# Tying the modulation products of a partial-product stage to its own products, and spreading a norm two half tiles later

## The chip, the core and the metric

The kernel is one program on one core of a Trainium2 chip. The core has a matrix engine (TensorE, PE in the profile, with its weight loads as PEld), a vector engine (DVE), a scalar engine (ACT), a general engine (GpSimd, POOL) and a queue that issues transfers from memory (SyncE, SP). The metric is the device time of one launch in microseconds (us), the median over runs of the same program. For the kernel before it is 3037.05 us over three runs, which lay between 3035.22 and 3038.11.

Each engine works through its own list of instructions in a fixed order. That order is made when the program is compiled: a scheduler goes through the instructions as the Python program emitted them, estimates when each would be ready, and puts an instruction ahead of one emitted earlier where the earlier one would still have to wait. An ordering can be forced with `tc.issue_after(ins)`: every instruction emitted inside the block on the engine of `ins` then comes behind `ins` in that engine's list. It is an order alone, not a wait.

## What is computed

The reference is a two-layer backbone over 256 latent and 256 context tokens with 2048 channels. Layer 0 mixes tokens by pooling, layer 1 by neighbourhood attention, and each is followed by a gated feed-forward network (FFN) with 5504 hidden channels. All of it is in float32. What matters here is layer 0:

```python
ml = (silu_c @ w_mod[i] + b_mod[i]).reshape(B, 6, 1, D)
a_lat = modulate(rms_norm(h, norm1_g[i]), ml[:, 0], ml[:, 1])
y_lat = pool_mix(a_lat, pool_w[j], pool_b[j], pool_scale[j])
h = h + ml[:, 2] * y_lat
h = h + ml[:, 5] * conv_ffn(modulate(rms_norm(h, norm2_g[i]), ml[:, 3], ml[:, 4]),
                            ffn_w_gate[i], ffn_w_up[i], ...)
```

The modulation `silu_c @ w_mod` is a product of one vector per stream with about 100 MB of weights per layer, so it is mostly a matter of fetching weights. Two streams (latent and context) go through the same weights. The second RMS norm needs the sum of squares over all 2048 channels of the mixed `h`, so its scale is known only when the last channel group is mixed.

## The kernel before

**The partial stage.** The mixer works on four groups of 512 channels. As soon as a group is mixed, its share of the first FFN products can be computed, without waiting for the others and without the norm's scale, which is multiplied in later. The loop `for g in range(4)` (L745) does this for the first eight gate and up columns (`NS = 8`). For each group, `partial` (L660) runs 16 tiles: eight gate or up columns in two blocks of four, gate before up. One tile is 12 products, in four triples over the group's channel blocks `A[4g]` to `A[4g+3]` (L705 to L707; `cg` and `cu` in the profile). A half tile is six of them. `between(half)` (L754) is called before each half tile, numbered 0 to 31 in a group, and emits everything else that has to happen meanwhile.

**The modulation.** `mod_pe` (L227) makes one chunk of 512 modulation channels: four pieces, each of two weight tiles of 512 KB (`wm` in the profile). Every second piece it emits one set of eight modulation products (L240, `mod`), called a pair below because it covers two pieces; the profile counts 16 records for it, because each instruction is recorded twice. After the fourth piece ACT copies the sum out (L255, `modev`), and four transposes (L262, `modt`) and small DVE operations finish the chunk's vector. For the last three chunks (`ch > 20`) there is one set of four products for each piece. `need(n)` pushes this generator to its n-th step; `between` calls it with a count that grows by about five for every eight half tiles. In group `g` the shift that the product `pw` (L687) reads is done at step `20 * g + 21`.

The list `behind_of` (L224) holds instructions behind which `mod_pe` puts its products and transposes. The mixer of the first group fills it; it is cleared before the partial stage (L741), so that within the partial stage the scheduler may put modulation products anywhere.

**Loads and rooms.** All weights go through one SP queue in the order of the program. They land in rooms: six tiles of their own and some tiles of `A` lent for a time (`LENT`, `lend`). A load waits until the last reader of its room is done, and all later loads wait behind it.

**Banks.** Products land in banks of PSUM. The tag `d` has three, used in turn by the tiles of `cg` and `cu`, by `pw`, by the transposes (`modt`, `ptg`, `ptu`) and by the norm. The modulation products have one bank of their own (`m`).

**The second norm.** In the last group (`g == 3`), before half tile `NRH` = 3, `n2.rstd()` (L377) emits the whole of the norm's end: 16 small products that sum the squares over partitions (L382, `n2s`), a reduction and a scaling on DVE (L385, L386), a power on POOL (L387, `n2v`), four diagonals on DVE (L390, `n2d`), and one product that spreads them over all partitions (L392, `n2b`). ACT copies that into `rstd` (L759). `need(20 * g + 21)` follows. From then on `normalise` makes the FFN's input of one channel block every second half tile (L403, L405, L406), twelve blocks within the stage and the last four after it, and `late` multiplies stored partial products by the scale on POOL (L461).

Of the kernel before, what the change touches and what calls it, by code (L numbers as in the profile page):

```python
# [17 lines left out]
P = 128  # L18
# [41 lines left out]
def kernel(ctx: ExitStack, tc: tile.TileContext, xT, cxT, wmod, wg, wu, wd, wp,  # L60
# [263 lines left out]
    class Norm:  # L324
# [50 lines left out]
            return pb  # L375

        def rstd(self):  # L377
            nj = self.n // P
            ps = bank("d", f"{self.name}s")
            for i, sq in enumerate((self.acc, self.last)):  # L380
                for j in range(nj):
                    nc.tensor.matmul(ps[:, 2 * j + i : 2 * j + i + 1], sq[:, P * j : P * j + P], ones[:, 0:1],  # L382
                                     start=True, stop=True)
            v = main.tile([P, 4], F32, tag="normv", bufs=2, name=f"{self.name}v")[:, :nj]
            nc.vector.tensor_reduce(out=v, in_=ps[:, 0 : 2 * nj].rearrange("p (j a) -> p j a", a=2), axis=AX.X, op=ALU.add)  # L385
            nc.vector.tensor_scalar(v, v, 1.0 / D, EPS, op0=ALU.mult, op1=ALU.add)  # L386
            nc.gpsimd.tensor_tensor(v, v, minus_half[:, :nj], op=ALU.pow)  # L387
            dg = self.pool.tile([P, 512], F32, tag="t2", name=f"{self.name}d")
            for j in range(nj):
                nc.vector.tensor_scalar(dg[:, P * j : P * j + P], ident, v[:, j : j + 1], None, op0=ALU.mult)  # L390
            pb = bank("d", f"{self.name}b")
            nc.tensor.matmul(pb[:, : self.n], ones, dg[:, : self.n], start=True, stop=True)  # L392
            return pb

    A = {}
# [34 lines left out]
    with ExitStack() as ph0:  # L430
# [64 lines left out]
        with ExitStack() as phs:  # L495
# [50 lines left out]
            def need(n):  # L546
                while done[0] < n:
                    next(pump0, None)
                    done[0] += 1
# [110 lines left out]
            def partial(g, sh, between):  # L660

                step = 0
                for fa in range(0, NS, 4):
                    for q, (nm, wsrc) in enumerate((("g", wg), ("u", wu))):
# [12 lines left out]
                        for j in range(4):  # L677
                            f = fa + j
                            between(2 * step)
                            if j == (3 if fa == 0 and q == 0 else 0):  # L680
                                need(20 * g + 21)
                                assert g in READY
                                pw = bank("d", f"pw{nm}{g}_{fa}")
                                for i in range(4):
                                    for jj, (t, n) in enumerate(ts):
                                        t3 = t.rearrange("p (f c) -> p f c", c=512)
                                        nc.tensor.matmul(pw[32 * i : 32 * i + 32, 256 * jj : 256 * jj + 256], sh[:, i, :],  # L687
                                                         t3[:, :, P * i : P * i + P], start=True, stop=True,
                                                         tile_position=(0, 32 * i))
                                ev = f0.tile([P, 512], F32, tag="t2", name=f"pe{nm}{g}_{fa}")  # L690
                                nc.scalar.copy(ev, pw)
                                used(ts)
                            if f >= NC:
                                if g == 0:
                                    HELD[f, q] = bank("gu", f"c{nm}_{f}")
                                ps = HELD[f, q]
                                first, final = g == 0, g == 3
                            else:
                                ps = bank("d", f"c{nm}{g}_{f}")
                                first = final = True  # L700
                            hi, lo = parts[j // 2]
                            for i in range(4):
                                c = 512 * (j % 2) + P * i
                                xh, xl = flat(A[4 * g + i][:, 0]), flat(A[4 * g + i][:, 1])
                                nc.tensor.matmul(ps, hi[:, c : c + P], xh, start=(first and i == 0), stop=False)  # L705
                                nc.tensor.matmul(ps, hi[:, c : c + P], xl, start=False, stop=False)
                                nc.tensor.matmul(ps, lo[:, c : c + P], xh, start=False, stop=(final and i == 3))  # L707
                                if i == 1:
                                    between(2 * step + 1)
                            step += 1  # L710
                            if f >= NC:
                                continue
                            if g == 0:
                                if q == 0:
                                    PART[f] = act_tile(f"part{f}", F32)
                                nc.scalar.copy(PART[f][:, q], ps)
                            else:
                                nc.vector.tensor_tensor(PART[f][:, q], PART[f][:, q], ps, op=ALU.add)
# [26 lines left out]
            for g in range(4):  # L745
                if g < 3:
                    lend((range(8, KT), [*range(12, KT), *range(4)], range(8))[g])
                mix = mixer(g + 1) if g < 3 else None
                todo = [20 * g + 20 + n for n in STEPS] if g < 3 else []
                last = [14]  # L750
                F = {}
                rstd = n2.acc

                def between(half):  # L754
                    need(min(20 * g + LEAD + RATE * (half + 1) // 32, 20 * g + LEAD + PMAX))
                    if (g, half) in LENT:
                        lend(LENT[g, half])
                    if g == 3 and half == NRH:
                        nc.scalar.copy(rstd, n2.rstd())  # L759
                        late_norm.append(rstd)  # L760
                        need(20 * g + 21)
                    if todo and done[0] > todo[0] and half >= last[0] + 2:
                        last[0] = half
                        todo.pop(0)
                        next(mix)
                    k = (half - NRH) // 2
                    if g == 3 and 0 <= k < 12 and (half - NRH) % 2 == 0:
                        normalise(0, 3, h_of, both, rstd, f0, range(k, k + 1), keep=F)
                    if g == 3 and half == 24:
                        EARLY[NC] = late(NC, (0,))[0]  # L770
                    if g == 3 and half in GATES:
                        e = GATES.index(half)
                        acts[e], _ = gate0(e, *late(e))

                partial(g, shs[g % 2], between)
                for n in todo:
                    need(n)
                    next(mix)
            need(97)
            in_turn.clear()  # L780
            nbank[0] = 0
            A.update(F)
# [766 lines left out]
```

## Time and profile before

| What | us |
|---|---|
| median of three runs | 3037.05 |
| the profiled execution, its own time | 3037.08 |
| its span, first to last instruction | 3035.3 |
| TensorE busy in the span | 2972.4 (98%) |
| DVE busy | 1943.6 (64%) |
| ACT busy | 1380.5 (45%) |
| POOL busy | 833.1 (27%) |

The profile gives times in us from the start of the span. A row of a timeline has the start, the length, the engine, the line, the operation, what it writes and reads, and, in square brackets, how long the engine stood idle before it and what ended that. A row of a window has the length of the window, the busy time of PE, PEld, DVE, ACT and POOL with the number of instructions in brackets, the granted TensorE clock as a share of full speed, the share of time in which the DMA engines were busy, and GB/s. Rows of the chain of waits have a start, a length and a name.

### The profile page before, as it was taken

How to read it: one execution, taken by the hardware profiler on the slowest of the kernel's cores; microseconds unless marked ns; L12 is line 12 of the kernel's file. 1: busy time of each engine (PE TensorE's matmuls, PEld its weight loads, DVE VectorE, ACT ScalarE, POOL GpSimd, SP SyncE). 2: the span in 40 equal slices, each digit the busy share in tenths (PEclk: the TensorE clock that was granted, in tenths of full speed). 3: DMA queues.
4: the chain of work that ended last, by engine and by line, in shares of the span. 5: the costliest groups of instructions: out<-in, count | busy, mean ns of one | idle time of the engine just before them, and what ended most of it. 6: DMA issues, size and time to landing. Idle time of an engine off the chain costs nothing.

```text
span 3035.3 us, 40942 instructions
## 1 busy us (share of the span) xinstructions
PE 2972.4 (98%) x15132; PEld 2414.0 (80%) x15132; DVE 1943.6 (64%) x2782; ACT 1380.5 (45%) x2237; POOL 833.1 (27%) x819
## 2 busy tenths in 40 slices
PE   5999999999999999999999999999999999999998
PEld 2666568888888888888888887878888888888887
DVE  5455664386584857758485657474778666666666
ACT  4433454323333242333434534343556666566665
POOL 0000213303123030311305002020002566566665
PEclk9999999999999999999999999999999999999999
DMA  9798563374665847566482333333345555555563
GB/s 395 290 366 306 209 209 103 109 252 146 208 197 168 245 140 236 156 205 203 156 254 82 127 100 122 107 120 112 106 158 195 185 193 191 190 183 187 183 192 119
DMA packets 178935, 561.81 MB, mean 185 GB/s; under 512 B 17712, under 2 KB 22576, under 8 KB 178736
## 3 DMA queue, kind: packets, MB, share of 16 engines
q1 hardware_dynamic: 178736, 559.19, 56.5%
q8 instruction: 120, 1.97, 0.3%
q14 instruction: 79, 0.65, 0.1%
HBM read 557.03 MB, written 2.10 MB: 184 GB/s over the span
## 4 chain that ended last, share of the span: by engine, by line
PE 88%; issue 6%; DMA 2%; POOL 1%; DVE 1%; ACT 1%; SPq 0%; DVEq 0%; POOLq 0%; ACTq 0%
PE d L863 5%; PE d L864 5%; PE d L865 5%; PE u L1070 5%; PE g L1070 5%; PE d L1123 4%; PE g L807 4%; PE g L805 4%; PE g L806 4%; PE u L807 4%; PE u L805 4%; PE u L806 4%; PE u L1073 3%; PE g L1073 3%; PE d L1127 2%
## 5 line engine op out<-in xcount | busy, mean ns | idle before, releaser
L876 POOL TENSOR_TENSOR hl<-hl,dy 128x256 f32<-128x256 f32 x160 | 146.1, 913 | 945.8 <-ACT dy L875 945.6
L1139 POOL TENSOR_TENSOR hl<-hl,dy 128x256 f32<-128x256 f32 x320 | 332.1, 1075 | 188.3 <-ACT dy L1137 186.0
L300 DVE SCALAR_TENSOR_TENSOR macc<-wm,sc,macc 128x512 f32<-128x512 f32 (+1 forms) x360 | 328.7, 943 | 75.3 <-DMA wm<-wmod 74.3
L875 ACT ACTIVATE dy<-d,modT 128x256 f32<-128x256 f32 x320 | 133.1, 469 | 187.3 <-PE d L865 168.9
L876 POOL TENSOR_TENSOR hc<-hc,dy 128x256 f32<-128x256 f32 x160 | 129.4, 809 | 0.0
L174 DVE TENSOR_TENSOR wd_2l<-wd,wd_2h 128x1024 fp32r<-128x1024 f32 (+1 forms) x44 | 55.7, 1271 | 108.1 <-ACT wd_2h L172 106.9
L1137 ACT ACTIVATE dy<-d,modT 128x512 f32<-128x512 f32 x160 | 104.5, 684 | 43.0 <-PE d L1127 41.4
L240 PE MATMUL mod<-wm,sc 128*32 128x512 f32 x768 | 99.6, 629 | 9.9 <-DMA wm<-wmod 9.9
L1225 POOL TENSOR_TENSOR rk<-rk,rp 128x256 f32<-128x256 f32 x16 | 14.8, 926 | 324.0 <-DVE rk L1224 225.6
L174 DVE TENSOR_TENSOR wd_3l<-wd,wd_3h 128x1024 fp32r<-128x1024 f32 (+1 forms) x44 | 53.4, 1234 | 77.1 <-ACT wd_3h L172 75.7
L635 POOL TENSOR_TENSOR hl<-hl,pz 128x256 f32<-128x256 f32 x12 | 9.8, 820 | 286.9 <-ACT pz L633 286.9
L174 DVE TENSOR_TENSOR wd_1l<-wd,wd_1h 128x1024 fp32r<-128x1024 f32 (+1 forms) x44 | 53.7, 1225 | 53.3 <-ACT wd_1h L172 53.3
L172 ACT CAST wd_1h<-wd 128x1024 fp32r<-128x1024 f32 (+1 forms) x44 | 45.3, 1031 | 72.3 <-PE u L806 47.1
L174 DVE TENSOR_TENSOR wd_0l<-wd,wd_0h 128x1024 fp32r<-128x1024 f32 (+1 forms) x44 | 54.5, 1247 | 36.9 <-ACT wd_0h L172 36.9
L1314 ACT ACTIVATE sb<-sb,nm 128x512 f32<-128x512 f32 x64 | 46.3, 723 | 58.9 <-DVE nm L1310 57.3
L172 ACT CAST wd_0h<-wd 128x1024 fp32r<-128x1024 f32 (+1 forms) x44 | 45.0, 1031 | 54.5 <-PE u L1070 29.1
L1102 DVE TENSOR_TENSOR actb<-sgb,actb 128x256 fp32r<-128x256 f32 x43 | 50.8, 1180 | 26.0 <-ACT actb L1101 26.0
L480 ACT ACTIVATE sg<-g 128x512 f32<-128x512 f32 x43 | 27.2, 632 | 88.4 <-DVE g L477 88.3
L863 PE MATMUL d<-act,wd_2h 128*128 128x512 f32 x172 | 67.1, 390 | 0.0
L864 PE MATMUL d<-act,wd_2h 128*128 128x512 f32 x172 | 66.9, 389 | 0.0
L865 PE MATMUL d<-act,wd_2l 128*128 128x512 f32 x172 | 66.9, 389 | 0.0
L864 PE MATMUL d<-act,wd_0h 128*128 128x512 f32 x172 | 66.9, 389 | 0.0
(1778 smaller groups left out, 9304.8 us busy)
## 6 DMA issues: line engine op xcount, KB each, us to landing
wm<-wmod SPq DMA_DIRECT2D x384, 512.0 KB, 6.5
wd<-wd SPq DMA_DIRECT2D x168, 512.0 KB, 4.4
wg<-wg SPq DMA_DIRECT2D x156, 512.0 KB, 4.7
wu<-wu SPq DMA_DIRECT2D x156, 512.0 KB, 4.6
wv<-wv SPq DMA_DIRECT2D x32, 512.0 KB, 4.0
wk<-wq SPq DMA_DIRECT2D x32, 512.0 KB, 3.9
wq<-wq SPq DMA_DIRECT2D x32, 512.0 KB, 3.8
wo<-wo SPq DMA_DIRECT2D x32, 512.0 KB, 4.4
```

The lines of the kernel that those rows point to most:

```text
L174: eng.tensor_tensor(lo[:, :n], t[:, :n], hi[:, :n].bitcast(F32), op=ALU.subtract)
L300: nc.vector.scalar_tensor_tensor(acc[s], v, sc2[:, k, s : s + 1], acc[s], op0=ALU.mult, op1=ALU.add)
L805: nc.tensor.matmul(ps, hi[:, c : c + P], xh, start=(k == 0), stop=False)
L806: nc.tensor.matmul(ps, hi[:, c : c + P], xl, start=False, stop=False)
L807: nc.tensor.matmul(ps, lo[:, c : c + P], xh, start=False, stop=(k == KT - 1))
L863: nc.tensor.matmul(ps, hi[:, o : o + P], xh, start=(i == 0), stop=False)
L864: nc.tensor.matmul(ps, hi[:, o : o + P], xl, start=False, stop=False)
L865: nc.tensor.matmul(ps, lo[:, o : o + P], xh, start=False, stop=(i == n - 1))
L876: nc.gpsimd.tensor_tensor(h_of(s)[:, k, :], h_of(s)[:, k, :], y[:, s], op=ALU.add)
L1070: nc.tensor.matmul(ps, hi[:, c : c + P], flat(B[k]), start=(k == 0), stop=False)
L1073: nc.tensor.matmul(ps[:, T:], lo[:, c : c + P], B[k][:, 0], start=False, stop=(k == KT - 1))
L1139: nc.gpsimd.tensor_tensor(hl[:, k, :], hl[:, k, :], y[:, q], op=ALU.add)
```

## The change

It has two parts. First, `partial` writes into `behind_of` the last product of each triple as it is emitted, so that modulation products and their transposes come behind the partial product that precedes them in the program. The list is cleared after the stage. Second, the norm's end is cut in two. The sums, the power and the diagonals are still emitted before half tile 3, and `need(20 * g + 21)` now follows them directly. The spreading product and the copy into `rstd` are emitted before half tile 5, with the spreading product behind the partial product before it. Each `normalise` step of the last group is emitted two half tiles later: the first before half tile 5 instead of 3, the twelfth before 27 instead of 25.

```diff
         def rstd(self):
+            self.diagonal()
+            return self.spread_all()
+
+        def diagonal(self):
             nj = self.n // P
...
                 nc.vector.tensor_scalar(dg[:, P * j : P * j + P], ident, v[:, j : j + 1], None, op0=ALU.mult)
+            self.dg = dg
+
+        def spread_all(self, last=()):
             pb = bank("d", f"{self.name}b")
-            nc.tensor.matmul(pb[:, : self.n], ones, dg[:, : self.n], start=True, stop=True)
+            with ExitStack() as behind:
+                for x in last:
+                    behind.enter_context(tc.issue_after(x))
+                nc.tensor.matmul(pb[:, : self.n], ones, self.dg[:, : self.n], start=True, stop=True)
             return pb
...
-                                nc.tensor.matmul(ps, lo[:, c : c + P], xh, start=False, stop=(final and i == 3))
+                                ins = nc.tensor.matmul(ps, lo[:, c : c + P], xh, start=False, stop=(final and i == 3))
+                                behind_of[:] = [ins.ins]
...
                     if g == 3 and half == NRH:
-                        nc.scalar.copy(rstd, n2.rstd())
+                        n2.diagonal()
+                        need(20 * g + 21)
+                    if g == 3 and half == NRH + 2:
+                        nc.scalar.copy(rstd, n2.spread_all(behind_of))
                         late_norm.append(rstd)
-                        need(20 * g + 21)
...
-                    k = (half - NRH) // 2
+                    k = (half - NRH) // 2 - 1
...
             need(97)
+            behind_of.clear()
             in_turn.clear()
```

## The prediction

> **What bounds the kernel now.** I read the page first (busy time by engine), then windows over the groups of the partial stage, then the chain of waits around the second norm, then the timelines of PE, DVE and ACT there. The page's first block, and windows over the third group, the last group in pieces, and the handover to the FFN:
>
> ```profile
> PE 2972.4 (98%) x15132; PEld 2414.0 (80%) x15132; DVE 1943.6 (64%) x2782; ACT 1380.5 (45%) x2237; POOL 833.1 (27%) x819
> ```
>
> ```profile
> 245.00:326.00 81.00, 80.60 (x472) 52.93 (x464) 46.50 (x91) 27.01 (x47) 2.86 (x4) 1.00 0.86 322
> 326.00:417.00 91.00, 82.93 (x478) 48.70 (x478) 63.95 (x123) 46.01 (x94) 22.14 (x17) 0.96 0.69 238
> ...
> 341.00:351.00 10.00, 5.82 (x23) 1.82 (x23) 3.81 (x8) 2.28 (x3) 1.02 (x1) 0.66 0.98 340
> ...
> 357.00:413.00 56.00, 55.62 (x315) 33.71 (x317) 45.36 (x84) 32.44 (x65) 15.32 (x10) 1.00 0.66 230
> ...
> 419.00:430.00 11.00, 11.00 (x43) 8.86 (x43) 11.00 (x21) 8.88 (x18) 0.00 (x0) 0.85 0.64 196
> ```
>
> PE bounds the kernel, and the stage too: 80.60 of 81 us in the third group, while the transfers have room (0.86). The last group takes 91 us with less mixing in it, and its loss sits in one place: from 341 to 351 PE is busy for 5.82 us at a clock of 0.66. The chain of waits there, then PE's timeline:
>
> ```profile
> 334.01 11.08 DMA wm<-wmod
> ...
> 345.18 3.64 PE mod L240 x16
> 348.82 1.95 PE n2b L392 x2
> ```
>
> ```profile
> 327.13 3.64 PE L240 MATMUL mod<-wm,sc 128*32 128x512 f32 x32
> 330.70 0.66 PE L721 MATMUL ptu<-ident,peu 128*128 128x128 f32 x4
> 331.12 0.70 PE L705 MATMUL cg<-Ad,wcg_0h 128*128 128x512 f32 x2
> ...
> 338.61 1.92 PE L240 MATMUL mod<-wm,sc 128*32 128x512 f32 x16
> 345.18 3.64 PE L240 MATMUL mod<-wm,sc 128*32 128x512 f32 x16 [4.64 <-DMA wm<-wmod]
> 348.75 2.02 PE L392 MATMUL n2b<-n2d,ones 128*128 128x512 f32 x2
> 350.61 0.60 PE L262 MATMUL modt<-ident,modev 128*128 128x128 f32 x4
> 350.96 0.48 PE L705 MATMUL cg<-Ad,wcg_0h 128*128 128x512 f32 x1
> ...
> 355.63 1.09 PE L687 MATMUL pwg<-wcg,sh 128*32 128x256 f32 x16 [1.65 <-ACT A L405]
> ...
> 361.20 0.50 PE L705 MATMUL cu<-Ad,wcu_0h 128*128 128x512 f32 x1
> ...
> 366.55 0.39 PE L707 MATMUL cu<-Ad,wcu_0l 128*128 128x512 f32 x1
> ```
>
> After two tiles (24 products, 331.12 to 338.61 with the norm's 16 sums) come two pairs of chunk 20. In the program they belong before half tiles 6 and 9, behind 36 and 54 products. The scheduler hoisted them; the second had no data until 345.09 (334.01 + 11.08), and the spread, the transposes of chunk 15 and the third tile stand behind it. Those transposes come late too: the chunk's last pair ended at 330.77, but their bank apparently follows the spread's in turn, and `pw` then waits 1.65 us for the shift they make.
>
> **The change, part by part.** Unit prices from these rows: a product is 5.35 / 23 = 0.233 us (361.20 to 366.55, 23 steps), so a tile is 2.8; a pair at full clock is about 1.85 (the 327.13 row: two in 3.64); transposes before a product 0.35 (350.61 to 350.96). Spreading costs 1.05 at full clock, by the first norm's spread:
>
> ```profile
> 26.65 1.12 PE L392 MATMUL n1b<-n1d,ones 128*128 128x512 f32 x2
> 27.70 1.92 PE L240 MATMUL mod<-wm,sc 128*32 128x512 f32 x16
> ```
>
> *The last group, cost first.* The 327.13 row is both pairs of chunk 15. The second belongs behind 18 products, so the tie takes it out of the place where PE waited for this group's channels anyway:
>
> ```profile
> 329.46 0.50 ACT L645 ACTIVATE Ad<-hc,modT 128x256 fp32r<-128x256 f32 x1
> ...
> 333.77 0.47 DVE L646 SCALAR_TENSOR_TENSOR Ad<-hc,modT,Ad 128x256 fp32r<-128x256 f32 x1
> ```
>
> PE is free at 327.13 + 1.85 + 0.42 (`ptu`) = 329.4, and the first product can start at 329.46 + 0.50 = 330.0. The low parts end at 334.24, when 18 products (4.2 us) are through, so DVE does not hold them. Then 24 products (5.6), the sums (7.49 - 5.6 = 1.9) and the pair (1.85) end at 339.35, where they ended at 338.61 before: 0.75 us lost.
>
> *The last group, gain.* From there: transposes of chunk 15 (0.35), the third tile (2.8), the first pair of chunk 20 (1.85; its data landed before 338.61), the spread (1.05): `pw` starts at 345.4 instead of 355.63. The second pair is then still owed, 1.85, and comes behind 54 products, near 353, with its data there since 345.09. Gain: 355.63 - 345.4 - 1.85 = **8.4 us**, if the spread is ready by 344.35. That hangs on DVE:
>
> ```profile
> 337.94 0.16 DVE L385 TENSOR_REDUCE n2v<-n2s 128x4 f32<-128x8 f32 x1
> 342.39 1.22 DVE L174 TENSOR_TENSOR wcu_0l<-wcu,wcu_0h 128x1024 fp32r<-128x1024 f32 x1 [4.30 <-ACT wcu_0h L172]
> 343.54 0.16 DVE L386 TENSOR_SCALAR n2v<-n2v 128x4 f32<-128x4 f32 x1
> ...
> 345.34 0.86 DVE L390 TENSOR_SCALAR n2d<-ident,n2v 128x128 f32<-128x128 f32 x4
> ```
>
> The scaling needs 2.66 us to the last diagonal (343.54 to 346.20), but stood behind a weight split (`wcu_0l`) that waited for its load. If DVE's list keeps that order, the diagonals end at 346.2 again, the spread waits 1.85 us, and the gain is 6.5. If not, the sums end near 338.6, the diagonals near 341.5, and nothing waits. I take the second, since the loads of `wcu` use rooms that the second pair of chunk 15 frees, and that pair ends 4 to 5 us later than before; the split should fall behind the scaling in the list. The split itself is needed at the fifth tile, near 351.
>
> *The third group.* Here too the second pair of its chunk (14) filled a wait for the channels (PE, then ACT):
>
> ```profile
> 244.24 1.93 PE L240 MATMUL mod<-wm,sc 128*32 128x512 f32 x16
> 246.09 0.74 PE L705 MATMUL cg<-Ad,wcg_0h 128*128 128x512 f32 x2
> ...
> 250.53 0.39 PE L705 MATMUL cg<-Ad,wcg_0h 128*128 128x512 f32 x1
> ```
>
> ```profile
> 245.26 0.49 ACT L645 ACTIVATE Ad<-hc,modT 128x256 fp32r<-128x256 f32 x1
> ```
>
> By 250.53 + 0.23 = 250.76 PE had done 20 products and the pair. Tied, the pair leaves PE waiting until 245.26 + 0.49 = 245.75; at full rate 21.5 products are done by 250.76, 0.35 us more, against 1.85 owed: **1.5 us lost** (bounds 0 and 1.85). In groups one and two the first pair of the group stays where it is, since nothing or only the group before precedes it; the others move by at most six products among products that are ready: 0.
>
> *Everything else that moves.* Pairs that come later free their rooms later, by at most 18 products (4.2 us). SP's queue then waits longer, with loads for all behind it. In the third group no pair made PE wait (80.60 of 81 us busy), and a load's delay is about that of the pair that uses it, so I put this at 0. If that cover is gone, each us of lateness is a us of PE. The `normalise` steps move by two half tiles on DVE and ACT; DVE is busy 45.36 of 56 us from 357 to 413, and its first reader is the FFN after 417: 0. The new line for the tie costs no instruction.
>
> **Sum.** 8.4 - 1.5 = 6.9 us off the profiled execution's 3037.08 (1.8 of it outside the span of 3035.3; the median, 3037.05, is the same to 0.03): **3030.2 us**. Own range of this case: with a hole that costs nothing and the wait before the FFN gone (1.29, below) 3027.4; with the full 1.85 lost and two slow starts (1.6 each, next) 3033.7.
>
> The clock is where a page bears on it. The pair took 3.64 instead of 1.92 after 4.64 us of idleness; but so did the start of the FFN go slow after shorter waits:
>
> ```profile
> 417.44 0.50 PE L805 MATMUL g<-A,wg_8h 128*128 128x512 f32 x1 [1.29 <-ACT wg_8h L172]
> ...
> 418.70 0.68 PE L807 MATMUL g<-A,wg_8l 128*128 128x512 f32 x1 [0.53 <-DVE wg_8l L174]
> ...
> 421.73 0.63 PE L805 MATMUL g<-A,wg_8h 128*128 128x512 f32 x1
> ```
>
> Eight products at 0.43 instead of 0.23 cost 1.6 us there. The Trainium skill, TensorE: Matmul & The Clock Gate, "Part 1: The HAM clock gate", says that the array falls to half clock after an idle window of about 3.4 us. By that rule the new holes (1.5 us and less) cost only themselves and the sum stays 3030.2. By the 417.44 row each could cost 1.6 more, and the sum would be 3033.4. I take the first, because the idle 1.65 us at 354 was followed by products at full speed.
>
> **The rivals.**
>
> *A. The spread waits.* DVE's list keeps the split in front, or the wait becomes another's: the spread runs at 346.2, the third group's loss stays: 3037.1 - 6.5 + 1.5 = 3032.1, and 3033.7 with a slow start. For it: the order of before. Against it: the later rooms. Chance 0.15.
>
> *B. The end gives it back.* After half tile 13 only six rooms are left, and the last twelve sets of modulation products go round in a circle of room, load, set. If that circle and not PE times the last third, the stage ends at 417 as before and PE waits longer at 417.44; what remains is the third group's loss: 3038.6. For it: SP's queue waits for modulation products more than for anything else. Against it: PE is busy 55.62 of 56 us there, so the loads come in time.
>
> ```profile
> SPq L154 <- PE mod L240: 164.1, 38, 20.4
> ```
>
> That is the wait of SP's queue up to 430 us, with the number of times and the longest. Chance 0.15.
>
> *C. Slower: DVE at the handover.* From 419 to 430 DVE is busy 11.00 of 11 us with the last four `normalise` blocks, splits and gates, on which the FFN's first products depend. Before that it has these gaps left:
>
> ```profile
> 415.75 0.19 DVE L264 TENSOR_REDUCE modT<-modt 128x8 f32<-128x32 f32 x1 [2.44 <-PE modt L262]
> ...
> 417.42 1.23 DVE L174 TENSOR_TENSOR wg_8l<-wg,wg_8h 128x1024 fp32r<-128x1024 f32 x1 [1.28 <-ACT wg_8h L172]
> ```
>
> If DVE is the bound there, an earlier PE brings nothing, and the two last steps moved behind their old place (four DVE passes of 0.48, 1.9 us each) come on top: 3.8 + the 1.5 of the third group + a slow start of 1.6, on 3037.1: 3044.0. It decides once more than the 3.7 us of gaps are filled. For it: the normalise work cannot start earlier by more than the spread does. Against it: until 412 DVE follows PE rather than leads it. Chance 0.20.
>
> **How the numbers follow.** My forecast has 0.50. Two tenths of a per cent, 6.1 us, is about what a measurement of this kernel can tell from no change, so faster is under 3031.0 and slower over 3043.1. Faster: 0.36 of the forecast's 0.50 and 0.04 of A: 0.40. Within: 0.14 of the forecast, 0.11 of A, 0.12 of B: 0.37. Slower: C's 0.20 and 0.03 of B: 0.23. The range reaches from 3027, the forecast's good end, to 3042, past B and most of the way to C.
>
> **What would show it.** No modulation set between the 24th product and the spread waits for a transfer; the third tile stands before the spread; `pw` of the last group starts near 345.4 + 1.5 = 346.9; the second pair of chunk 20 stands behind 54 products; DVE's scaling follows its reduction directly (rival A if not); holes of about 0.6 and 1.5 us before the first products of groups four and three; the FFN's first product at about 410 (B and C if at 417 or later, told apart by whether the wait before it ends with `wg_8` landing or with `A`). The prediction is wrong if pairs in groups two or three begin to wait for transfers, or if the FFN that follows changes its own length by more than a us or two.

## The result and the profile after

The changed kernel is slower. Its median is 3043.61 us (3040.67 to 3050.29, 20 runs) beside 3037.18 us for the kernel before (3030.55 to 3040.96, 20 runs): a ratio of 1.0024, 95% interval 1.0017 to 1.0031. The prediction was 3030.2, with a range from 3027 to 3042.

The profiled execution of the changed kernel took 3041.02 us, near the quick end of its runs, with a span of 3039.2. Below are the windows over the same stretches as before (PE, PEld, DVE, ACT and POOL busy, granted clock, DMA share, GB/s):

```profile
341.00:351.00 10.00, 10.00 (x66) 6.00 (x66) 5.66 (x15) 2.68 (x3) 2.13 (x2) 1.00 0.46 177
357.00:413.00 56.00, 53.14 (x290) 31.29 (x291) 44.25 (x80) 30.76 (x63) 12.34 (x9) 0.97 0.71 244
419.00:430.00 11.00, 8.88 (x31) 6.85 (x32) 10.84 (x20) 9.34 (x18) 0.00 (x0) 0.84 0.64 204
```

The change did what it was made for: from 341 to 351 PE is now busy for 10.00 us at full clock (5.82 at 0.66 before). But from 357 to 413 it is busy for 53.14 of 56 us (55.62 before), and from 419 to 430 for 8.88 of 11 (11.00 before). PE's timeline of the last group shows both the gain and the first new loss:

```profile
333.43 0.73 PE L715 MATMUL cg<-Ad,wcg_0h 128*128 128x512 f32 x2 [0.38 <-ACT Ad L655]
334.63 0.50 PE L716 MATMUL cg<-Ad,wcg_0h 128*128 128x512 f32 x1 [0.47 <-DVE Ad L656]
...
343.69 0.60 PE L262 MATMUL modt<-ident,modev 128*128 128x128 f32 x4
344.26 0.50 PE L715 MATMUL cg<-Ad,wcg_0h 128*128 128x512 f32 x1
...
347.20 1.92 PE L240 MATMUL mod<-wm,sc 128*32 128x512 f32 x16
349.06 1.13 PE L402 MATMUL n2b<-n2d,ones 128*128 128x512 f32 x2
350.11 1.09 PE L697 MATMUL pwg<-wcg,sh 128*32 128x256 f32 x16
...
357.93 0.80 PE L715 MATMUL cu<-Ad,wcu_0h 128*128 128x512 f32 x1 [2.32 <-DVE part L729]
```

The first 24 products, the sums and the tied pair end at 343.69 (338.61 before): 5.08 later, of which 3.4 come from the groups before (the transposes of chunk 19 stand at 329.95, before at 326.55). Then transposes, third tile, pair and spread run without a gap, and the shift's products start at 350.11 instead of 355.63. From 343.69 on, that is 10.6 us quicker. With the pair still owed (1.85) 8.75 are left, where the prediction had 355.63 - 345.4 - 1.85 + 0.75 = 9.1 from the same point. At the start of the fifth tile, 2.32 us of waiting for a bank and six products at 0.43 us (1.2 more than at full rate) take back 3.5 of it. What holds the bank is on DVE and POOL:

```profile
350.84 1.60 DVE L413 SCALAR_TENSOR_TENSOR nrm<-hl,modT,n2acc 128x256 f32<-128x256 f32 x1 [2.29 <-ACT n2acc L773]
...
353.80 1.50 DVE L413 SCALAR_TENSOR_TENSOR nrm<-hl,modT,n2acc 128x256 f32<-128x256 f32 x1
355.22 0.47 DVE L413 SCALAR_TENSOR_TENSOR nrm<-hc,modT,n2acc 128x256 f32<-128x256 f32 x1
355.61 1.66 DVE L416 SCALAR_TENSOR_TENSOR A<-nrm,modT,A 128x256 fp32r<-128x256 f32 x4
357.20 0.68 DVE L729 TENSOR_TENSOR part<-part,cg 128x512 f32<-128x512 f32 x1
```

```profile
350.88 4.12 POOL L471 TENSOR_TENSOR part<-part,n2acc 128x512 f32<-128x512 f32 x3 [3.91 <-ACT n2acc L773]
```

The addition of the fourth tile (L729) ends at 357.88, and PE's next product starts at 357.93. The addition stands behind the first two `normalise` steps, whose first three passes take 1.5 to 1.6 us each instead of 0.47, exactly while POOL makes three `late` multiplications of 1.37. Because the third tile now precedes the spread, three partial sums are ready for POOL when the norm arrives; before there were two.

Followed through the stage, this execution is 3.4 us behind the kernel before at the transposes of chunk 19, 5.1 behind at the end of the sums, 5.5 ahead at the shift's products (with a pair still owed), 0.3 behind at the next transposes (367.06, before 366.78), 1.8 behind at the FFN's start (419.25, before 417.44) and 3.9 behind at the end.

A second profile of the same kernel shows an execution from the other side of its median (3046.31 us, span 3044.3). This is the view of PE's waits from 85 to 430 us (total, number, longest), first of the kernel before, then of this second execution of the changed one:

```profile
PE mod L240 <- DMA wm<-wmod: 4.6, 1, 4.6
PE cg L705 <- ACT Ad L645: 2.4, 1, 2.4
PE pwg L687 <- ACT A L405: 1.6, 1, 1.6
```

```profile
PE cg L715 <- ACT Ad L655: 3.6, 3, 1.9
PE cu L715 <- DVE part L729: 2.3, 1, 2.3
PE cg L715 <- DVE n2v L389: 2.3, 1, 2.3
PE u L819 <- ACT wu_8h L172: 1.9, 1, 1.9
PE pwg L697 <- DVE sh L541: 1.8, 1, 1.8
...
PE pwu L697 <- DMA wcu<-wu: 1.4, 1, 1.4
```

The two waits of the old hole (4.6 and 1.6) are gone. In their place stand a larger hole for the channels (`Ad`, 1.2 more) and five waits that the kernel before did not have: 2.3 + 2.3 + 1.9 + 1.8 + 1.4 = 9.7 us. The `n2v` and `sh` waits are absent from the first, quicker execution, and the last of the five is 0.5 us there. In all, PE waits 17.4 us in this stretch, before 11.9: that is 5.5 of the 9.0 us between the two spans. Another 2.5 are a slow start near 70 us, in front of everything that the change moves; the last section shows it.

### The profile page after: what moved, and what is told of

The parts are those of the page before. It is cut to its first block, busy times and chain, and to the rows that moved or that the text cites. A ratio compares the mean times of both kernels' runs of the same rounds, so it can differ in the third digit from the quotient of the medians.

```text
span 3039.2 us, 40934 instructions
## 1 busy us (share of the span) xinstructions
PE 2975.6 (98%) x15132; PEld 2413.6 (79%) x15132; DVE 1945.2 (64%) x2782; ACT 1380.0 (45%) x2237; POOL 833.0 (27%) x819
## 4 chain that ended last, share of the span: by engine, by line
PE 81%; issue 9%; POOL 2%; DVE 1%; ACT 1%; DMA 0%; DVEq 0%; POOLq 0%; SPq 0%; ACTq 0%
PE d L877 5%; PE d L878 5%; PE u L1084 5%; PE d L879 5%; PE g L1084 5%; PE d L1137 4%; PE g L821 4%; PE g L819 4%; PE g L820 4%; PE u L819 4%; PE u L820 4%; PE u L821 4%; PE u L1087 3%; PE g L1087 3%; PE d L1141 2%
## 5 line engine op out<-in xcount | busy, mean ns | idle before, releaser
L877 PE MATMUL d<-act,wd_0h 128*128 128x512 f32 x172 | 66.9, 389 | 0.0
L878 PE MATMUL d<-act,wd_0h 128*128 128x512 f32 x172 | 66.9, 389 | 0.0
```

The costliest lines, as they stand in the source:

```text
L877: nc.tensor.matmul(ps, hi[:, o : o + P], xh, start=(i == 0), stop=False)
L878: nc.tensor.matmul(ps, hi[:, o : o + P], xl, start=False, stop=False)
```

## The experiments

The starting theory: the ties take pairs out of holes and the second part brings the gain (T); the first `normalise` steps, slowed by POOL, hold up a bank (D). Against it: the ties are free and the moved normalise steps cost everything (N). Medians, with the difference to the median of the kernel before on the same chip:

| kernel | median us (runs) | difference | ratio, 95% interval |
|---|---|---|---|
| the change | 3043.6 (20) | +6.4 | 1.0024 (1.0017 to 1.0031) |
| the change again | 3045.8 (8) | +7.8 | 1.0025 (1.0015 to 1.0036) |
| tie alone | 3047.8 (9) | +10.4 | 1.0033 (1.0023 to 1.0043) |
| second part alone | 3032.4 (11) | -5.0 | 0.9984 (0.9975 to 0.9993) |
| the same again | 3034.6 (11) | -3.4 | 0.9990 (0.9981 to 0.9998) |
| second part, POOL waits | 3030.8 (11) | -4.7 | 0.9982 (0.9973 to 0.9991) |
| the same again | 3030.7 (8) | -7.3 | 0.9976 (0.9966 to 0.9985) |
| tie from the third tile | 3037.1 (11) | -0.3 | 1.0001 (0.9992 to 1.0010) |
| tie in the last group only | 3040.9 (11) | +5.4 | 1.0016 (1.0007 to 1.0024) |
| tie but for the tail | 3042.1 (12) | +6.6 | 1.0017 (1.0008 to 1.0026) |
| the change, POOL waits | 3043.1 (11) | +5.7 | 1.0018 (1.0009 to 1.0027) |
| the change, norm first | 3042.9 (11) | +4.9 | 1.0024 (1.0015 to 1.0033) |
| the change, pairs earlier | 3048.1 (5) | +12.6 | 1.0040 (1.0027 to 1.0053) |

### The tie alone

```
+                                behind_of[:] = [ins.ins]
...
                     if g == 3 and half == NRH:
                         nc.scalar.copy(rstd, n2.rstd())
                         late_norm.append(rstd)
                         need(20 * g + 21)
```

> Only the tie: modulation products and their transposes behind the partial product before them; norm, spread and normalise steps stand as in the kernel before. Theory T (the tie takes pairs out of the holes at the starts of groups, and they are owed later): the transposes of chunk 19 are 3 us or more later than before (326.55 there, 329.95 with the whole change), the last group's sums about 5 us later; the spread still waits for its diagonals (about 4 us idle), so nothing of the 8.7 us comes, and the time is 3037 to 3042. Rival N (the tie costs nothing, the moved normalise steps cost it all): the transposes of chunk 19 within 0.5 us of 326.55 and the time at or under 3037.

It is 10 us slower than the kernel before, more than T had (3037 to 3042). The transposes of chunk 19 stand at 332.73, 6.2 us later than before, of which about 2.5 are a slow start near 70 us. The hole around the spread, which the second part was to remove, grew, as PE's timeline of this kernel shows:

```profile
353.41 2.08 PE L402 MATMUL n2b<-n2d,ones 128*128 128x512 f32 x2 [6.79 <-DVE n2d L394]
```

The pair that used to stand in this hole is now held back behind the third tile, and the diagonals come later than before. Rival N is out: the tie costs time without any moved step.

### The second part alone

```
+                                products[:] = [ins.ins]
...
+                        nc.scalar.copy(rstd, n2.spread_all(products))
```

> Only the second part: sums and diagonals at half tile 3, the spread behind the third tile's first products, normalise two half tiles later; no tie on the modulation products. Theory T: the transposes of chunk 19 at 326.5, as before; the first pair of chunk 20 goes before the third tile, the second waits some 1 to 2 us for its data in front of the spread, and the last group's products of the shift start near 348 (355.63 before): 7 us gained with no pair owed. Theory D (the first normalise steps hold up the addition whose bank PE needs): the fifth tile then starts 2 us or more after PE was free, with a slow start, and 4 of the 7 us are gone; the time is 3033 to 3037. Without D it is near 3029. Rival N: the time stays at 3041 or over, as with the whole change.

Faster than the kernel before, twice (-5.0 and -3.4). In the profile (in which the transposes of chunk 19 stand 0.9 us later, at 327.43) the shift's products start at 347.88, 7.75 us earlier than before, with no pair owed: both pairs of chunk 20 run before the spread, in time that PE would have waited anyway. Then the stall of theory D comes here too, on PE's timeline:

```profile
355.69 0.80 PE L716 MATMUL cu<-Ad,wcu_0h 128*128 128x512 f32 x1 [2.31 <-DVE part L730]
```

By the next transposes 4.0 us of the gain are left (362.82, before 366.78), and 3.6 at the FFN's start (413.83, before 417.44). The sum of the two parts alone, 10.4 - 5.0 = 5.4, is the 6.4 of the change within what the runs can tell: by the medians the parts do not hurt each other, and the first one costs two to three times what the second one brings.

### The tie from the third tile on

```
-                                behind_of[:] = [ins.ins]
+                                behind_of[:] = [ins.ins] if step > 1 else []
```

> The whole change, but the tie holds only from the third tile of each group on, so that pairs can go into the holes at the groups' starts. Theory T: the transposes of chunk 19 within 1 us of 326.55, the spread free of waits, the shift's products near 346 (350.1 with the whole change), and the time 3 to 5 us under that of the whole change: 3038 to 3041 beside its 3043.6, profiled span 3034 to 3036. Rival N: no more than 1 us better than the whole change.

With pairs free to enter the holes at the starts of groups, 6 to 7 us come back: 3037.1. The transposes of chunk 19 stand at 327.08 (329.95 in the change). The expectation was too small, and its claim that the spread would not wait was wrong: with a single pair of chunk 20 ahead of it, the spread waits 2.59 us for its diagonals. What is left above the second part alone, 3.1 to 4.7 us by the table, belongs to the tie from the third tile on; besides this wait its profile has two at the stage's end (1.9 and 1.4 us), which the part on the tail takes up.

### Theory D: POOL's multiplications held back

```
-                    nc.gpsimd.tensor_tensor(r, r, late_norm[0], op=ALU.mult)
+                    mul = nc.gpsimd.tensor_tensor(r, r, late_norm[0], op=ALU.mult).ins
+                    if q == 0 and f < 3:
+                        tc.add_manual_dep(mul, FOURTH[0].name, ...)
```

`FOURTH` is the last group's addition of the fourth tile (f = 3).

> The whole change, with POOL's first three multiplications by the norm made to wait for the addition of the last group's fourth tile. Theory D with POOL as the cause (a DVE pass that begins while POOL multiplies takes 1.5 us instead of 0.47): the first eight DVE passes of normalise take about 0.45 each and end before 355, the addition of the fourth tile follows its product at once, PE does not wait before the fifth tile (2.32 us in the whole change) and starts at full clock, and about 4 us come back at that point, 2 or more of them at the end. Rival L (the order in DVE's list alone holds the addition up): the passes are short but PE still waits 1.5 us or more. Rival I (POOL is not it): the DVE passes stay at 1.5 us.

The mechanism is as D says. DVE's and POOL's timelines in this kernel:

```profile
356.67 0.48 DVE L413 SCALAR_TENSOR_TENSOR nrm<-hl,modT,n2acc 128x256 f32<-128x256 f32 x1 [2.29 <-ACT n2acc L779]
...
360.02 0.69 DVE L733 TENSOR_TENSOR part<-part,cg 128x512 f32<-128x512 f32 x1
...
360.92 1.51 DVE L413 SCALAR_TENSOR_TENSOR nrm<-hl,modT,n2acc 128x256 f32<-128x256 f32 x1
```

```profile
360.84 5.60 POOL L472 TENSOR_TENSOR part<-part,n2acc 128x512 f32<-128x512 f32 x4 [8.04 <-DVE pug L745]
```

The passes take 0.48 us, and turn to 1.51 the moment POOL starts at 360.84, where nothing of PE depends on them. PE goes on to the fifth tile without a wait. The time hardly shows it (+5.7 beside +6.4): the 2 us or more that were expected at the end did not come. Nor can the price be read from this run, since its profile has a wait of 2.34 us before the third tile, which is new beside the first profile of the change and led to theory W below.

### The same on the second part alone

> The second part alone (no tie), with POOL's first three multiplications by the norm waiting for the addition of the last group's fourth tile. Theory D: the stall before the fifth tile (2.31 us idle and six products at half rate in the second part alone) is gone and the 7.7 us won at the shift's products stay: FFN start 3 us or more before that of the second part alone (413.83), time 3027 to 3030, better than every kernel so far. Rival: POOL's multiplications, now later, stall DVE at the next tiles instead and the time stays at 3032 to 3033.

3030.8, just over the expected 3030. Beside the kernel before of its own chip it was no better than the second part alone (-4.7, and -5.0), while its profile showed the fifth tile following at once and the FFN's start at 408.96 (413.83). So both went once more onto one chip:

> The second part alone, beside the next run on one chip: 5 us under the kernel before, as it was, since its waits (second pair of chunk 20 on its load, fifth tile on the bank) are in its order and not in luck.

> The second part alone with POOL's multiplications waiting, beside the run above on one chip. Theory D says 2 to 4 us under the second part alone (the stall of 2.3 us and at times a slow start go), 7 to 9 under the kernel before. If what the profile shows is given back in most executions, it is within 1 us of the second part alone, as the medians of the first pair of runs had it once the kernel before is subtracted on each chip (-5.0 and -4.7).

There the difference is 3.9 us (3030.7 and 3034.6), as D has it. In the profiles the way from the transposes of chunk 19 to the FFN's start is 4.3 us shorter in the first pair of runs and 2.7 in the second. The mechanism is shown in both; its price in the time rests on the second pair alone. The waits left in this kernel, from the same view as above:

```profile
PE cg L720 <- ACT Ad L660: 2.4, 1, 2.4
PE mod L241 <- issue: 1.5, 1, 1.5
```

This kernel is faster than both the kernel before and the changed one: 0.9976 (0.9966 to 0.9985) and 0.9982 (0.9973 to 0.9991) of the kernel before.

### Where the tie costs: last group, and tail

```
-                                behind_of[:] = [ins.ins]
+                                behind_of[:] = [ins.ins] if g == 3 else []
```

The spread stays behind its partial product, as in the change.

> The whole change with the tie in the last group alone. If the last group's own hole (1.7 us) and its tail (some 3 us) are what the tie costs, the time is 4 to 5 us above the second part alone: 3036 to 3038, and the transposes of chunk 19 stand within 1 us of where the second part alone has them. What is then left to the whole change's 3043.6, about 6 us, is the cost of the tie in the groups before. If it all comes from the last group, the time is 3042 or more.

3040.9: by the differences in the table 9 to 10 us above the second part alone, where 4 to 5 were expected. So most of the tie's cost comes from the last group, and 1 to 2.4 us from the three before it (the first profile, with 3.4 us at the transposes of chunk 19, puts somewhat more there). Its profile has the transposes of chunk 19 in their old place (326.26), and then these waits, which the second part alone does not have:

```profile
PE cg L716 <- DVE n2v L390: 2.2, 1, 2.2
PE u L821 <- ACT wu_8h L172: 1.9, 1, 1.9
PE pwu L698 <- DMA wcu<-wu: 1.8, 2, 1.4
```

The second and third belong to the tail:

```
-                                behind_of[:] = [ins.ins]
+                                behind_of[:] = [ins.ins] if g < 3 or step < 8 else []
```

> The whole change, with the tie dropped from the ninth tile of the last group on. Theory R (sets tied late free their rooms late, SP loads late, and the last weight tile and the FFN's first weights land late): the waits of 0.2 to 1.4 us on transfers before the last shift's products go, FFN start 1.5 to 3 us earlier relative to the middle of the group, and the time 3040 to 3042. Rival H (only the holes at the starts of groups cost): no change from the whole change, 3043 to 3044.

With the tie gone from the ninth tile on, the profile has neither of them any more, and the way from the spread to the FFN's start takes 67.2 us, where the two profiles of the change have 70.2 and 71.7. In the time nothing is settled: by the ratios it is 2 us better (1.0017, the change 1.0024), by the differences in the table between 1.2 better and 0.2 worse. How the wait for the weights (`wcu`) arises is seen in the change's own timeline of PE:

```profile
394.07 1.92 PE L240 MATMUL mod<-wm,sc 128*32 128x512 f32 x16
396.70 0.66 PE L262 MATMUL modt<-ident,modev 128*128 128x128 f32 x4 [0.71 <-ACT modev L255]
...
399.62 0.59 PE L697 MATMUL pwu<-wcu,sh 128*32 128x256 f32 x2 [0.52 <-DMA wcu<-wu]
```

Tied, the last two sets of chunk 22 run back to back at 394.07, in front of their own transposes. In the kernel before they ran at 392.77 and 394.66, and the set ahead of them at 387.00 instead of 391.48. A room comes free only when its set is done, so SP issues the modulation load behind that set at 392.61 instead of 388.13, and then `wcu_4` at 395.20 instead of 393.90.

The wait of 1.9 us before `u` is of another kind. DVE's and PE's timelines of the change at the FFN's start:

```profile
420.29 2.35 DVE L174 TENSOR_TENSOR wg_8l<-wg,wg_8h 128x1024 fp32r<-128x1024 f32 x2
```

```profile
421.85 0.50 PE L819 MATMUL u<-A,wu_8h 128*128 128x512 f32 x1 [1.87 <-ACT wu_8h L172]
```

In the kernel before, the split of `wg_8` stands in front of the four `normalise` passes (417.42, the passes from 419.26 on), and PE goes on with it. Here the passes come first (418.63 to 420.29), and PE's list has a product on `wu_8h` instead, for which it waits. The lists have this order in all seven profiles with the tie in force up to the end of the last group (but for the run with pairs asked for earlier), the tie alone among them, and not in the second part alone. So it comes with the tie and not with the moved steps.

### Theory W: the reduction behind the split

In three kernels with the tie in force at the start of the last group, the third tile waited for the norm's reduction: 2.34, 2.20 and 1.66 us (in the tie alone it is the spread that waits). The first profile of the change has no such wait. DVE's timeline there:

```profile
342.90 1.23 DVE L174 TENSOR_TENSOR wcu_0l<-wcu,wcu_0h 128x1024 fp32r<-128x1024 f32 x1 [0.39 <-ACT wcu_0h L172]
344.04 0.16 DVE L389 TENSOR_REDUCE n2v<-n2s 128x4 f32<-128x8 f32 x1
```

The reduction stands behind the split of `wcu_0` in DVE's list, and ended (344.20) just as PE was ready (344.26). In the second part alone the same list has the reduction in front:

```profile
338.82 0.16 DVE L390 TENSOR_REDUCE n2v<-n2s 128x4 f32<-128x8 f32 x1
342.18 1.22 DVE L174 TENSOR_TENSOR wcu_0l<-wcu,wcu_0h 128x1024 fp32r<-128x1024 f32 x1 [3.19 <-ACT wcu_0h L172]
```

So the hypothesis was that the tie, which puts a pair in front of the sums, makes the scheduler place the split first, and that the change was lucky in its first profile. The lists agree with it: the reduction stands behind the split in five of the six kernels with the tie there (in front with pairs asked for earlier), and in front of it in every kernel without.

> The changed kernel itself once more, on the chip of the three that follow, for a second profile. Theory W (the first profile of it, 3041.0 us where the median is 3043.6, shows a lucky execution: the second low part of the split of wcu_0 came just in time there): the third tile of the last group waits 1.5 to 2.5 us for the norm's reduction, which stands behind that split on DVE, as it did in five of the six kernels with the tie in force at the start of the last group; time 3042 to 3045. Rival: no wait there again, and the 6 us lie elsewhere.

It is so: the second execution waits 2.26 us there. The split stands at 348.68 (`wcu` landed late), the reduction at 349.82, and the third tile begins at 350.04. In the third group the shift's copy stands behind the same kind of split (259.54 to 263.19), and the products of the shift wait 1.78 us. The count in the expectation was off: four kernels of the six had waited, the tie alone at the spread; the change had not, nor the run with pairs asked for earlier.

```
+                            hold[:] = [n2.diag] if (g, q, fa) == (3, 1, 0) else []
                             parts = split(ts, f"wc{nm}{g}_{fa}", keep=True)
+                            hold.clear()
```

`n2.diag` is the last diagonal; PE's and ACT's orders stay as they are.

> The whole change, with the split of the last group's wcu_0 put behind the norm's diagonals, so that reduction, scaling and diagonals stand ahead of it in DVE's list; nothing else moves, on PE or ACT. Theory W: no wait before the third tile or the spread; 2 us or more better than the whole change beside it, 3039 to 3042. Rival: the wait turns up before the fifth tile, which needs the split, or nothing waited there in the first place, and the time is that of the whole change within 1 us.

The wait is gone. DVE's timeline:

```profile
345.25 0.17 DVE L389 TENSOR_REDUCE n2v<-n2s 128x4 f32<-128x8 f32 x1
...
347.15 0.87 DVE L394 TENSOR_SCALAR n2d<-ident,n2v 128x128 f32<-128x128 f32 x4
...
348.07 2.57 DVE L174 TENSOR_TENSOR wcu_0l<-wcu,wcu_0h 128x1024 fp32r<-128x1024 f32 x2
```

From the third group's last shift products to the last group's first (303.8 to 355.63 in the kernel before) PE takes 43.06 us instead of 45.55 in the run beside it, and the split is still in time for the fifth tile. The medians agree with that (3042.9, 3045.8), but the ratios, 1.0024 and 1.0025, do not: the place is shown, the 2.5 us at the end are not.

### Pairs asked for earlier

```
-LEAD = 18
+LEAD = 20
```

> The whole change, with every modulation pair asked for two steps (one pair) earlier in the program. Theory P (the tie costs because the program's places are later than those to which the scheduler had moved the pairs; one pair earlier fills the holes again and frees rooms earlier): 3 us or more better than the whole change, 3036 to 3040, with the holes at the starts of groups three and four under 1 us. Rival Q (any fixed place costs, since pairs then wait for their loads): 3043 or more, with pairs that wait for transfers.

The holes are filled, as theory P has it: the third group's first product follows the transposes at once. Yet the time is 12.6 us over the kernel before. PE's waits from 85 to 420 us say why P falls:

```profile
PE pwu L697 <- DVE pug L739: 4.7, 2, 2.5
PE modt L262 <- ACT modev L255: 4.2, 5, 1.4
PE pwu L697 <- DMA wcu<-wu: 2.6, 2, 2.0
```

A fixed place moves the waits, as rival Q says, though for pairs no transfer was waited for: the transposes and the weights are what comes late.

## Why the prediction was wrong, point by point

**The step that failed** is setting to 0 most of what the change moves. The sum had 8.4 us of gain and 1.5 of loss. What it put at 0 (the moved `normalise` steps, the later loads, the lists of the other engines) came back as five new waits of PE, 9.7 us in the second execution, and the tie alone made the kernel 10.4 us slower.

**The gain in the last group** came as predicted in the first execution: 8.75 us against 9.1 from the end of the sums on, third tile first, the spread at full clock, the second pair of chunk 20 behind 54 products. That execution was lucky. In the second, nearer the median of its runs, the wait for the reduction leaves 6.5 (the shift's products 8.7 us behind the end of the sums, at 355.88).

**"The split should fall behind the scaling in the list"** was wrong. The list kept the split in front (342.90, 344.04), as rival A had it. But A put the wait at the spread and priced it at 1.85 us off the gain; it fell on the third tile, apparently because its bank is the one in which the sums stood, and it is 2.3 us in the second execution and near nothing in the first. That the tie itself, by moving the sums back by one pair, turns the list against the norm was not seen.

**The holes** were of the right kind and too small. In the last group 0.75 us was predicted and 1.7 measured (5.08 - 3.4). In the third group 1.5 was predicted and 1.9 measured in the first profile (the shift's products 2.87 late at 259.87, the transposes ahead of them 1.0); in the second it is 3.8, with the wait for the shift. **Groups one and two**, put at 0, cost about 1 us: the same instructions take 19.31 instead of 18.89 and 19.33 instead of 18.82 us between two shifts, with no wait at all, apparently because a pair that is moved away from `pwu` or `pwg` adds a seam of its own.

**"The `normalise` steps ... 0"** is the largest single term put at 0. The working asked whether DVE has time on average (45.36 of 56 us) and whether the reader is far off. It did not ask what stands behind these steps in DVE's list: the addition that frees PE's next bank. The second part alone loses 2.7 to 4.3 us to it up to the FFN's start, by the two pairs of profiles with and without POOL held back. The profile of before had the means to see it, one pass of 1.61 beside POOL's pair of multiplications (DVE, then POOL):

```profile
351.43 1.61 DVE L403 SCALAR_TENSOR_TENSOR nrm<-hl,modT,n2acc 128x256 f32<-128x256 f32 x1
```

```profile
351.47 2.71 POOL L461 TENSOR_TENSOR part<-part,n2acc 128x512 f32<-128x512 f32 x2 [6.68 <-ACT n2acc L759]
```

**"Pairs that come later free their rooms later ... 0"** failed in the tail. The cover that the prediction named, PE busy in the third group, said nothing of the last third of the last group, with six rooms. For the wait on the last `wcu` (0.5 us in the first execution, 1.4 in the second) rival B had the mechanism, but it took the end for a fixed limit instead of a cost of the tie. Its sign came up, the FFN's first product at 419.25 behind the landing of `wg_8`; but that wait is 1.36 us where it was 1.29 before, so the circle is not what took the gain. The wait of 1.9 us before `u` is in no part of the prediction: it comes from the order of the lists at the FFN's start, which the tie turned round.

**Rival C**, the slower one at 3044.0, met the time almost to the microsecond, with DVE as the engine that decides. The match is luck: C has none of the last group's gain and little of what took it back. Its place was only partly right: from 419 to 430 PE does lose 2.1 us (8.88 of 11), 1.9 of it before `u`, while DVE works through four normalise passes before the FFN's split. But the tie alone has that wait too, without any moved step, and most of the loss lies between 333 and 358 and in the tail. A forecast of 3030.2 is what is left if one counts what the change removes and sets nearly everything that it moves to zero.

**The clock.** Here the rule of the Trainium skill, TensorE: Matmul & The Clock Gate, "Part 1: The HAM clock gate", was taken over the row at 417.44, and the row was nearer. A wait of 2.3 us, shorter than the 3.4 us of that section, was followed by half-rate products in four of eight profiles that have it.

## What to carry to other kernels

An instruction moved on a busy engine is priced by what stands behind it in that engine's list, not by the engine's share of busy time: here an addition of 0.68 us that frees a bank cost PE 2.3. A tie that fixes the order of one engine can also turn round the lists of others, as it did here in two places on DVE, and a pair that seems misplaced may stand in a wait that has to be waited anyway; untie what fills holes, and tie only what must not go first. Of a change in two parts run each part alone: the second one, with POOL's work held back, gives 0.998 of the time before.

## What the runs showed of the hardware

**DVE and POOL.** A DVE pass with two operands in SBUF (L413) that starts beside a POOL multiplication takes 1.49 to 1.62 us instead of 0.47 to 0.49. One pass goes by for each POOL multiplication (1.37 us each in the change). An addition with one operand in a bank (L729) takes 0.67 to 0.69 in every case, three of them beside a POOL multiplication. The Trainium skill, SBUF — State Buffer, "SBUF: two separate sides", describes an exclusive lock that is held for a whole instruction, and the rows agree with it: in all fourteen profiles every slow pass ends 0.28 or 0.29 us behind the end of a POOL multiplication.

**The clock after the same wait.** At the start of the first group every kernel has the same order and the same waits, and yet runs at full or half rate, in PE's timeline of the first and second execution of the change:

```profile
67.34 0.66 PE L262 MATMUL modt<-ident,modev 128*128 128x128 f32 x4 [1.65 <-ACT modev L255]
69.62 0.73 PE L715 MATMUL cg<-Ad,wcg_0h 128*128 128x512 f32 x2 [1.63 <-ACT Ad L655]
70.28 1.92 PE L240 MATMUL mod<-wm,sc 128*32 128x512 f32 x16
```

```profile
67.94 0.66 PE L262 MATMUL modt<-ident,modev 128*128 128x128 f32 x4 [1.64 <-ACT modev L255]
70.22 1.22 PE L715 MATMUL cg<-Ad,wcg_0h 128*128 128x512 f32 x2 [1.62 <-ACT Ad L655]
71.37 3.64 PE L240 MATMUL mod<-wm,sc 128*32 128x512 f32 x16
```

Two waits of 1.6 us with 0.66 of work between them cost 2.5 us in the second case and nothing in the first. Nine of the fourteen profiles start slowly there: eight of the nine with a tie and one of the five without. Up to 67 us the orders of PE, ACT, DVE and POOL are the same in all fourteen, so the tie has no visible hand in it; whether the uneven count is chance stays open. Such starts can explain part of the 10 us by which the runs of one kernel differ, and they are why one profile of each is not enough here. The same section of the Trainium skill on the clock gate says that the window runs freely, and that the moment of the switch depends on where in it the first product lands; these two views are what that would look like.

**Loads after a pause.** When loads set in again in the last group, the second 512 KB load landed 1.8 us behind the first in the first execution of the change (337.38, 335.63) and 4.5 in the second (343.80, 339.27). The loads of `wcu` stand behind these two in SP's queue, so that this decides when `wcu_0` can be split. What makes the difference stays open.
